# Subtracting the low part of every projection weight tile on GpSimd instead of VectorE

## The chip, the core and the metric

The kernel runs on one core of one Trainium2 chip. The metric is device time in microseconds (us) of one execution; several executions of a kernel are timed and their median is taken. Engines are named as the profile names them: PE is TensorE's matmul and PEld its weight load, DVE is VectorE, ACT is ScalarE, POOL is GpSimd, SP is SyncE, which here only issues DMAs.

## The reference, cut to what matters

One layer over 2064 tokens (16 learned meta tokens, then 2048) of 1024 numbers each:

```python
h = rmsnorm(x, norm_g)
p = h @ w_in                       # 1024 x 8208: the combined projection
qkv, z, a, b, sc_b, sc_c, sc_h, sc_z = split(p)
q, k, v = silu(causal_conv4(qkv))  # 8 heads of 128; q and k L2-normalised
o = chunk_gated_delta_rule(q, k, v, g(a), beta(b))
o_dn = rmsnorm(o) * silu(z)
o_sc = sc_b * causal_conv3(sc_c * sc_h) * silu(sc_z)
out = rmsnorm(x + concat(o_dn, o_sc) @ w_out)[16:]
```

The delta rule is a recurrence along the tokens with a triangular solve in each chunk. All inputs and outputs are float32.

## The kernel before

**Three products for one.** Matrix products run in the type `fp32r`. To keep float32 accuracy each operand is split: a high part (the value rounded to `fp32r`, written by ACT) and a low part (the value less its high part, again in `fp32r`). A product is then high x high + low x high + high x low, summed in PSUM. For a weight tile the three buffers are `wr` (raw, as loaded), `wh` (high) and `wl` (low), each 128 x 1024; the pool has two of each. For the tokens they are `hh` and `hl`.

**Jobs.** The projection is cut into 128 jobs: two halves of the sequence (`hf` 0 and 1), each 64 jobs of 128 columns of `w_in`, eight for each of eight heads (k, q, v, z of the delta group, then c, h, b, z of the short convolution). A job runs over three groups of tokens (272 or 256, 384, 384 columns); in each `run_group` issues 24 matmuls into one PSUM tile `mm`: 16 with `wh`, then 8 with `wl`. After the last group of job j, `split_w(j + 2)` issues the split of the weights of job j + 2: ACT copies `wr` to `wh`, and the subtraction `wl = wr - wh` follows. The loading of the weights of job j + 4 into the buffer `wr` just read (`load_w`, a DMA of 512 KB on SP's queue) is issued behind the subtraction.

**Two ways for the subtraction.** `split_w` has an argument `eng`. Without it the subtraction is cut into two halves of 512 columns, which are put into the list `side`; `pump` takes from that list when the planner thinks that DVE has little queued (`LAG`), and `side_until` empties it up to the half that a matmul is about to need. With `eng=nc.gpsimd` it is one POOL instruction over all 1024 columns, issued at once, with `load_w` right behind it. Before the change POOL has four: jobs 0 and 1, from the prologue, and the two jobs at the start of the second half (`POOLED`). The other 124 are on DVE.

**The order.** It is written out by the program itself: a planner (`Model`) keeps a clock for each engine with a cost for every kind of instruction (in `cost`: POOL's is 0.12 + n/445 us for a `tensor_tensor` of n columns) and the generators in `streams` yield until the planner says that their inputs are ready. Between the matmuls of a job, `pump` lets these generators issue the delta rule of the heads: `delta_front` (decay matrix E, Gram matrices of k and q, with the splits `gw`), `delta_inverse` (a triangular solve in 31 rows of two DVE instructions each, on `prod` and `XT`), `delta_back` (merging of blocks, on `W`, `X`, `Q`), `delta_scan` (the recurrence, 8 chunks a head, each with the DVE instructions `yy` and `S` between matmuls into `rec`), `delta_out` (normalisation, on `os`, and the gate `zs`). Every engine executes its own instructions strictly in the order issued. The planner has no term for two engines that hinder each other.

**POOL's other work.** The powers that stand for reciprocal roots (`opy`, `kpy`, `pxy`), the masks of `E` and `prod`, and two or three columns at the head of each convolution's buffer (`raw`, `sc_u`).

**The end.** When the jobs are done, 32 units of 48 matmuls multiply the mixed tokens with `w_out`. Their splits use the same pool tags `wr`, `wh`, `wl`, by ACT and DVE in `load_mix`; the change doesn't touch them.

Of the kernel before, what the change touches and what calls it, by code (L numbers as in the profile page):

```python
# [173 lines left out]
def hybrid_trunk(  # L174
# [544 lines left out]
    def split_w(j, eng=None):  # L719
        if j >= len(jobs):  # L720
            return
        J = jobs[j]
        J.wh = vt(wp, [128, KT, 128], "wh", dt=F32R)
        J.wl = vt(wp, [128, KT, 128], "wl", dt=F32R)
        nc.scalar.activation(J.wh, J.wr, AF.Copy)

        if eng is not None:
            eng.tensor_tensor(out=J.wl, in0=J.wr, in1=J.wh, op=ALU.subtract)
            load_w(j + 2)
            done.add(("w", j))  # L730
            return

        def half(i):
            s_ = slice(4 * i, 4 * i + 4)
            nc.vector.tensor_tensor(out=J.wl[:, s_], in0=J.wr[:, s_], in1=J.wh[:, s_], op=ALU.subtract)
            if i == 1:
                load_w(j + 2)

        later(lambda: half(0))
        later(lambda: half(1), ("w", j))  # L740

    def run_group(j, g):
# [25 lines left out]
        if g == 2:  # L768
            if J.fin:
                J.fin()  # L770
            split_w(j + 2, nc.gpsimd if j + 2 in POOLED else None)

# [739 lines left out]
        for l_ in sj:  # L1512
            jobs += l_
    NJ = len(jobs)
    POOLED = (NJ // 2, NJ // 2 + 1)
    HJ = NJ // 2
    start(prologue0())
    pump()
# [145 lines left out]
```

## Time and profile before

| | us |
|---|---|
| median of 3 runs | 2280.11 |
| lowest and highest | 2278.43, 2284.24 |
| the profiled execution | 2277.27 |
| its span, first to last instruction | 2275.5 |
| mean granted clock of TensorE, as a share of full speed | 0.985 |

The profile is of one execution. Its span lacks 1.8 us of that execution's own time, and the execution is 2.8 us below the median. A busy engine in it is one that executes an instruction; the idle time of an engine before an instruction is put down to what the instruction waited for. Nearly every instruction has the line 118, that of the helper that records it, so groups are told apart by the tiles they write and read.

### The profile page before, as it was taken

To read this page: it belongs to the slowest core of one execution; us is meant where nothing else is said; L and a number is where in the kernel's file an instruction comes from. 1 tells how busy PE (TensorE), PEld (TensorE's weight loads), DVE (VectorE), ACT (ScalarE), POOL (GpSimd) and SP (SyncE) were. 2 spreads that over 40 slices of the span, in tenths; PEclk is the share of its full clock that TensorE was granted. 3 is DMA by queue.
4 is the path that set the end of the run, shared out by engine and by line. 5 is a ranking of instruction groups with operands and counts; after the bars stand their busy time and mean duration, and the time that the engine had idled before them with its cause. 6 is when DMAs were issued, how large, how long until landed. Compare 5 with 4: busy or idle time off the path is not lost. (4 is left out here: it accounts for less than half of the span.)

```text
span 2275.5 us, 38771 instructions
## 1 busy us (share of the span) xinstructions
PE 2192.7 (96%) x15024; PEld 2071.2 (91%) x15024; DVE 1463.7 (64%) x4027; ACT 863.8 (38%) x2078; POOL 186.7 (8%) x343
## 2 busy tenths in 40 slices
PE   6999999999999998899999999999999999999998
PEld 6998899999998898889999999999999998788886
DVE  4667866777677657486877676776776775434222
ACT  5542444343434342344434343434352425322111
POOL 4010101010101010010100101010101000000000
PEclk9999899999999999999999999999999999999999
DMA  6443336534434478534443454243436864655231
GB/s 141 73 81 71 62 77 92 77 69 86 83 60 72 83 83 68 101 76 71 68 80 61 75 60 83 52 77 52 77 52 65 62 92 145 217 166 177 83 102 56
DMA packets 256518, 194.90 MB, mean 86 GB/s; under 512 B 62005, under 2 KB 226366, under 8 KB 256334
## 3 DMA queue, kind: packets, MB, share of 16 engines
q1 hardware_dynamic: 256334, 192.42, 46.5%
q8 instruction: 118, 1.93, 0.3%
q14 instruction: 66, 0.54, 0.1%
HBM read 156.58 MB, written 35.80 MB: 85 GB/s over the span
## 5 line engine op out<-in xcount | busy, mean ns | idle before, releaser
L118 PE MATMUL mm<-hh,wh 128*128 128x384 f32 (+3 forms) x3328 | 1046.3, 336 | 13.0 <-issue 6.7
L118 PE MATMUL mm<-hl,wh 128*128 128x384 f32 (+3 forms) x3328 | 1017.7, 327 | 0.0
L118 PEld LDWEIGHTS mm<-hh,wh 128*128 128x128 f32 x3328 | 630.4, 190 | 21.6 <-ACT hh L118 5.4
L118 PEld LDWEIGHTS mm<-hl,wh 128*128 128x128 f32 x3328 | 631.5, 191 | 16.5 <-issue 6.8
L118 PE MATMUL mm<-hh,wl 128*128 128x384 f32 (+3 forms) x3200 | 624.1, 327 | 6.9 <-DVE wl L118 6.9
L118 PEld LDWEIGHTS mm<-hh,wl 128*128 128x128 f32 x3200 | 512.0, 189 | 15.0 <-DVE wl L118 8.6
L118 DVE SCALAR_TENSOR_TENSOR acc<-raw,pcol,acc 128x384 f32<-128x384 f32 (+2 forms) x432 | 249.1, 580 | 76.3 <-ACT acc L118 70.9
L118 DVE TENSOR_TENSOR wl<-wr,wh 128x512 fp32r<-128x512 f32 x344 | 231.7, 694 | 100.9 <-ACT wh L118 58.8
L118 ACT ACTIVATE wh<-wr 128x1024 fp32r<-128x1024 f32 x176 | 185.7, 1055 | 106.1 <-PE mm L118 65.1
L118 DVE SCALAR_TENSOR_TENSOR prod<-nb,XT 128x8 f32<-128x8 f32 (+30 forms) x496 | 190.1, 383 | 24.4 <-DMA nb<-nbd 20.9
L118 DVE TENSOR_REDUCE XT<-prod 128x8 f32<-128x16 f32 (+30 forms) x496 | 147.2, 297 | 17.1
L118 ACT ACTIVATE raw<-mm 128x272 f32<-128x272 f32 (+2 forms) x144 | 65.7, 456 | 213.7 <-PE mm L118 213.1
L118 ACT ACTIVATE vn<-rec,cj 128x128 f32<-128x128 f32 x128 | 47.0, 367 | 226.3 <-PE rec L118 225.9
L118 ACT ACTIVATE sc_c<-mm 128x384 f32<-128x384 f32 (+4 forms) x99 | 45.1, 456 | 167.4 <-PE mm L118 167.3
L118 PE MATMUL mm<-oh,wh 128*128 128x512 f32 x256 | 101.9, 398 | 0.0
L118 PE MATMUL mm<-ol,wh 128*128 128x512 f32 x256 | 100.3, 392 | 0.0
L118 DVE TENSOR_TENSOR y<-mm,y 128x512 f32<-128x512 f32 x24 | 16.6, 692 | 115.9 <-PE mm L118 115.9
L118 POOL TENSOR_TENSOR opy<-mo,nhalf 128x4 f32<-128x4 f32 x32 | 35.7, 1116 | 648.6 <-DVE mo L118 592.7
L118 ACT ACTIVATE ojk<-y 128x512 bf16<-128x512 f32 x24 | 15.2, 632 | 191.6 <-DVE y L118 127.1
L118 DVE SCALAR_TENSOR_TENSOR yy<-rec,neg,vr 128x128 f32<-128x128 f32 x128 | 44.4, 347 | 60.8 <-PE rec L118 60.2
L118 ACT ACTIVATE acc<-mm,pcol 128x272 f32<-128x272 f32 (+2 forms) x144 | 78.2, 543 | 0.1
L118 DVE SCALAR_TENSOR_TENSOR S<-S,egl,rec 128x128 f32<-128x128 f32 x104 | 35.6, 343 | 61.0 <-PE rec L118 60.4
(244 smaller groups left out, 2596.1 us busy)
## 6 DMA issues: line engine op xcount, KB each, us to landing
wr<-in_w_in_dram SPq DMA_DIRECT2D x128, 512.0 KB, 9.0
wr<-mixd SPq DMA_DIRECT2D x48, 512.0 KB, 4.2
E<-gtd SPq DMA_DIRECT2D x16, 512.0 KB, 3.8
qd<-ged SPq DMA_DIRECT2D x16, 512.0 KB, 4.6
nb<-nbd SPq DMA_DIRECT2D x64, 128.0 KB, 4.3
mixd<-zs SPq DMA_DIRECT2D x32, 256.0 KB, 2.6
out_dram<-y SPq DMA_DIRECT2D x16, 512.0 KB, 2.7
mixd<-sc_y SPq DMA_DIRECT2D x32, 192.0 KB, 2.4
```

Of the source, the lines that this page charges most:

```text
L118: r = real(*args, **kw)
```

## The change

```diff
-    POOLED = (NJ // 2, NJ // 2 + 1)
+    POOLED = range(NJ)
```

`NJ` is 128. `POOLED` is read at one place, the last line of `run_group`: `split_w(j + 2, nc.gpsimd if j + 2 in POOLED else None)`. So for the jobs that had it on DVE (124 of them) the subtraction is now one POOL instruction of 1024 columns in place of two DVE halves of 512, the entries in `side` are gone, and `load_w(j + 2)` for that buffer is issued at once at the end of the job. Since the planner's clocks for DVE and POOL change with it, the order in which everything else is issued changes too.

## Rows read from the trace of the kernel before

**Rows 1.** The page, part 1: busy time, share and instructions of each engine.

```profile
PE 2192.7 (96%) x15024; PEld 2071.2 (91%) x15024; DVE 1463.7 (64%) x4027; ACT 863.8 (38%) x2078; POOL 186.7 (8%) x343
```

**Rows 2.** Stretches: busy us of PE, PEld, DVE, ACT, POOL; clock; DMA share; GB/s.

```profile
300.00:700.00 400.00, 396.01 (x2978) 385.28 (x2977) 282.39 (x856) 158.58 (x411) 35.75 (x67) 1.00 0.45 77
...
1000.00:1700.00 700.00, 696.94 (x5295) 680.61 (x5294) 505.69 (x1324) 291.86 (x727) 51.03 (x79) 1.00 0.41 67
```

**Rows 3.** PE's waits: us in total, times, longest.

```profile
PE mm L118 <- DVE wl L118: 6.9, 6, 4.0
```

**Rows 4.** Groups of instructions by shape: busy us, mean ns | idle before.

```profile
L118 DVE TENSOR_TENSOR wl<-wr,wh 128x512 fp32r<-128x512 f32 x344 | 231.7, 694 | 100.9 <-ACT wh L118 58.8 <-PE mm L118 35.8 <-PE rec L118 3.1
...
L118 POOL TENSOR_TENSOR wl<-wr,wh 128x1024 fp32r<-128x1024 f32 x4 | 9.5, 2381 | 16.9 <-ACT wh L118 16.9
```

**Rows 5.** DVE busy on tile wl alone, over the jobs' stretch; clock; DMA.

```profile
50.00:1905.00 1855.00, 170.48 (x250) 0.98 0.48 74
```

**Rows 6.** Timeline of POOL around 980 us: start, us, instruction.

```profile
974.84 2.39 POOL L118 TENSOR_TENSOR wl<-wr,wh 128x1024 fp32r<-128x1024 f32 x1 [7.71 <-ACT wh L118]
979.63 2.39 POOL L118 TENSOR_TENSOR wl<-wr,wh 128x1024 fp32r<-128x1024 f32 x1 [2.40 <-ACT wh L118]
981.96 0.22 POOL L118 COPY raw<-qcar 128x3 f32<-128x3 f32 x1
```

**Rows 7.** Timeline of DVE beside them.

```profile
975.28 0.69 DVE L118 TENSOR_TENSOR hl<-ta,hh 128x512 fp32r<-128x512 f32 x1 [1.39 <-ACT hh L118]
...
976.14 1.18 DVE L118 SCALAR_TENSOR_TENSOR prod<-nb,XT 128x80 f32<-128x80 f32 x1
...
978.90 0.15 DVE L118 SCALAR_TENSOR_TENSOR msm<-mnb,mXT 16x7 f32<-16x7 f32 x1
...
980.04 2.00 DVE L118 SCALAR_TENSOR_TENSOR msm<-mnb,mXT 16x8 f32<-16x8 f32 x1
```

**Rows 8.** Timeline of ACT: first, one middle and last of the 124 copies.

```profile
51.74 1.05 ACT L118 ACTIVATE wh<-wr 128x1024 fp32r<-128x1024 f32 x1
...
1425.78 1.06 ACT L118 ACTIVATE wh<-wr 128x1024 fp32r<-128x1024 f32 x1
...
1864.23 1.06 ACT L118 ACTIVATE wh<-wr 128x1024 fp32r<-128x1024 f32 x1 [3.50 <-PE mm L118]
```

**Rows 9.** Timeline of DVE behind the last two of these.

```profile
1427.11 0.40 DVE L118 SCALAR_TENSOR_TENSOR prod<-nb,XT 128x136 f32<-128x136 f32 x1
...
1865.45 0.16 DVE L118 SCALAR_TENSOR_TENSOR opt<-opt,mo 128x4 f32<-128x4 f32 x1
```

**Rows 10.** Three groups of DVE, by shape, that hand straight on to PE.

```profile
L118 DVE SCALAR_TENSOR_TENSOR yy<-rec,neg,vr 128x128 f32<-128x128 f32 x128 | 44.4, 347 | 60.8 <-PE rec L118 60.2
...
L118 DVE SCALAR_TENSOR_TENSOR S<-S,egl,rec 128x128 f32<-128x128 f32 x104 | 35.6, 343 | 61.0 <-PE rec L118 60.4
...
L118 DVE TENSOR_TENSOR gw<-q,gw 128x256 fp32r<-128x256 f32 x64 | 26.7, 418 | 0.0
```

**Rows 11.** Timeline of DVE: first and last of the 128 yy.

```profile
229.45 0.35 DVE L118 SCALAR_TENSOR_TENSOR yy<-rec,neg,vr 128x128 f32<-128x128 f32 x1
...
1938.16 0.35 DVE L118 SCALAR_TENSOR_TENSOR yy<-rec,neg,vr 128x128 f32<-128x128 f32 x1 [1.48 <-PE rec L118]
```

**Rows 12.** Timeline of PE: the matmuls that read these two.

```profile
231.23 0.38 PE L118 MATMUL rec<-yy,W 128*128 128x128 f32 x2
...
1939.55 0.38 PE L118 MATMUL rec<-yy,W 128*128 128x128 f32 x2
```

**Rows 13.** Three short stretches: columns as in the second group.

```profile
260.00:280.00 20.00, 14.54 (x66) 12.65 (x66) 18.68 (x53) 6.92 (x20) 1.25 (x1) 0.66 0.42 93
...
880.00:890.00 10.00, 5.06 (x20) 4.77 (x21) 9.62 (x30) 2.63 (x8) 0.00 (x0) 0.66 0.87 46
475.00:490.00 15.00, 13.23 (x91) 13.04 (x90) 10.75 (x54) 9.35 (x21) 1.30 (x3) 1.00 0.26 50
```

**Rows 14.** Waits of SP's DMA queue: us in total, times, longest.

```profile
SPq L118 <- DVE wl L118: 742.9, 151, 20.8
```

## The prediction, made before the changed kernel was run

> **What bounds the kernel now.** I read the page's busy shares first: PE is busy 96% of the span, DVE 64%, POOL 8% [rows 1]. Then the busy time by stretches, because a share of the whole span hides where the idle time lies: from 300 to 700 us PE idles for 4.0 of 400 us, from 1000 to 1700 us for 3.1 of 700 [rows 2]. In these stretches the matmuls are the time, and nothing that another engine does faster can shorten them. DVE idles there for 117.6 of 400 us and 194.3 of 700, that is 29% and 28% [rows 2]. Third, PE's own waits: in the whole execution PE waits for a low part of a weight on DVE six times, 6.9 us in all [rows 3]. So the subtractions that the change moves stand on the path for 6.9 us at most, though DVE spends 694 ns on each half [rows 4]. The reader should see that DVE is a loaded helper and not the bound, and that what counts is whether DVE's results for the delta rule come in time for the matmuls that are already queued in PE's fixed order.
>
> **What the change removes.** 124 jobs lose two DVE halves each: 248 x 694 ns = 172 us [rows 4], in line with the 170.5 us that DVE spends on `wl` between 50 and 1905 us [rows 5]. All of it lies beside PE's work but for the 6.9 us above; I count 0 for it directly, with 6.9 us of gain as the other end.
>
> **What it adds on POOL.** 124 subtractions of 2.381 us [rows 4] make 295 us, on an engine with 187 us of work [rows 1]. The copies of `wh` run from 51.7 to 1864.2 us [rows 8], so a job takes about 1812/124 = 14.6 us; copy and subtraction need 1.06 + 2.39 us of that, and the first matmul with this `wl` comes a whole job later. So PE should not wait for the subtraction itself: 0.
>
> **What it adds on DVE: being held.** Two of POOL's four subtractions ran beside a working DVE, from 974.84 and from 979.63 us, 2.39 us each [rows 6]. In the first, a DVE instruction with one input in PSUM (`hl<-ta,hh`) took its usual 0.69 us, but `prod<-nb,XT`, with both inputs in SBUF, took 1.18 us and ended at 977.32, right behind POOL's end at 977.23. In the second, `msm<-mnb,mXT`, at 0.15 us a little before, took 2.00 us and ended at 982.04, again with POOL (982.02) [rows 6, 7]. A larger `prod` (136 columns) takes 0.40 us undisturbed [rows 9]. So a DVE instruction that reads two operands in SBUF and begins during a POOL subtraction ends when POOL ends. The Trainium skill says the same (SBUF — State Buffer, section "Who interferes with whom"): such a DVE instruction contends with a GpSimd instruction that reads SBUF, and the loser blocks until the other is through. By that page the price is what is left of POOL's instruction, as these two rows have it; were the two engines independent, the sum below would lose its one positive term.
>
> I sized this by walking the timeline: for each of the 124 `wh` copies (the first, one between and the last are shown) [rows 8] a POOL subtraction of 2.39 us was laid right behind it, and the next DVE row with two inputs in SBUF, `wl` left out, was held until its end. Behind the copy at 1425.78 (ends 1426.84) POOL would run until 1429.28, and `prod` of 1427.11 would be held for 2.17 us; behind the last (ends 1865.29, POOL until 1867.73) `opt` of 1865.45 for 2.28 us [rows 8, 9]. In 20 of the 124 cases no such row begins in time. The sum over all is 189 us, 1.53 us a job; the two real cases, 0.8 us (1.18 less 0.40 at most for a smaller shape) and 1.85 us, have a mean of 1.3 us, or 164 us, and the ends are 0 and 124 x 2.39 = 296 us. I take 189: with 172 us removed, DVE gains nothing, and its work comes in gaps of up to 2.4 us which the planner doesn't know of.
>
> **What PE sees of it.** From the end of a `yy` to the matmul that reads it there are 231.23 - 229.80 = 1.43 us at the first and 1939.55 - 1938.51 = 1.04 us at the last of the 128; their median is 1.07 us [rows 11, 12]. A delay of DVE below that is free, and what lies above it stops PE. Of the 124 holds 92 are longer than 1.07 us, by 84 us in all. A delayed DVE catches up only in its idle time, 29% of the time [rows 2], so it is late by more than 1.07 us during 84/0.29 = 290 us. The DVE instructions that hand straight on to PE are 128 `yy`, 104 `S` and 64 pairs of `gw` [rows 10], 296 in 1855 us, one in 6.3 us; so 46 of them fall into late times, late by half of the mean excess (84/92/2 = 0.46 us): 21 us. This leaves out `os`, `X` and `W`. Moving every DVE row of the walk along, with catching up in the idle times, and letting PE wait where a matmul's input comes later than the matmul stands, gave 36 us at 56 places, 17 of them between 1000 and 1700 us, where PE now hardly waits. I take 32 us; the ends are 0 (no hold falls on a chain) and 84 (each does).
>
> **Clock.** PE's clock falls where PE is sparse for several microseconds: 0.66 from 260 to 280 us with 5.5 us of idle, 0.66 from 880 to 890; in a stretch with 1.8 us of idle (475 to 490) it stayed at 1.00 [rows 13]. The new waits are below 2.4 us and scattered, so I count 0; one more stretch of the first kind would cost 5.5 us of idle and 0.34 x 20 = 6.8 us of clock.
>
> **What it may give back.** In the two sparse stretches of rows 13 DVE is busy 18.7 of 20 and 9.6 of 10 us: PE has no matmul to issue because a head's delta rule is late. There are four such (also 725 to 740 and 770 to 780 us), with 17.8 us of idle and 0.34 x 55 = 18.7 us of clock. Fewer entries in `side` let the planner issue the solves earlier. But DVE's real load isn't less, so I take 6 us of the 36.
>
> **What is moved in the queues.** On POOL, the copies into the head of `raw` now wait for a subtraction, as the one at 981.96 us did [rows 6]; behind a late copy DVE's `acc`, and with it `prod` and `yy`, would be held. In the walk a few first readers stand before the copy's end, by less than 0.8 us: 0 to 4 us, taken as 0. POOL's powers and masks wait for up to 2.39 us more, and the planner knows it (its formula gives 2.42 us); 0. POOL in turn waits for `wh`, as ACT's copy ends it. On SP's queue `load_w` is issued earlier, and everything behind it waits until POOL has read `wr`: 1.06 + 2.39 us and ACT's queue behind a job's end, 4 to 5 us. Now SP waits for DVE's halves for 742.9/151 = 4.9 us a time [rows 14]. So 0, within 8 us either way, since the transfers of `nb` that start a solve stand in that queue.
>
> **Sum.** The profiled execution took 2277.3 us: + 32 - 6 = 2303 us. The median is 2.8 us above that execution: **2306 us**, 1.1% slower.
>
> **Rivals.** *The heads run ahead.* If the solves, freed of the halves in between, finish some 5 us earlier, the four sparse stretches vanish (-36 us), and if the chains, issued earlier, gain slack so that only a third of the holds' cost is left (+11 us), the time is 2280 - 25 = 2255 us; in part, up to 2272. It decides from the point where a job no longer waits for the scan of the head before last. For it: DVE is full there. Against it: the holds fall on just these instructions, `prod` above all. *Nothing moves.* The holds stay within the slack of 1.07 us or cancel against the relief: 2274 to 2287, say 2280 us. The Trainium skill has a sentence for this (Perfetto Trace Analysis, section "Optimizing Scalar/DVE Operations"): offloading between these two engines may not help, as they share a read port; the trace agrees so far as 172 us stand against 189. *The sparse stretches multiply.* Where DVE is already above 90% a hold isn't caught up, and a head's delta rule is late for the next job. Four more stretches of 12.3 us on top of the 32 give 2280 + 32 + 49 = 2361 us. For it: heads in the first half have the `msm` rows in addition. Against it: from 1000 to 1700 us DVE has 28% to spare.
>
> **How the numbers follow.** The forecast, 2288 to 2340 us, has 0.57, the multiplied stretches (above 2340) 0.08, nothing moved 0.16, the heads ahead 0.19. A measurement of this kernel can tell about 0.3% (7 us) from no change. So slower has 0.65, same 0.16, faster 0.19. The range that leaves out half of the two outer cases is 2262 to 2345 us.
>
> **What would show it.** In the profile after, DVE's busy time should be about as before (1464 - 172 + 189 = 1481 us) though 248 instructions are gone, with `prod`, `acc` and `junk` longer on average; POOL near 480 us; PE's waits for DVE `S`, `yy`, `gw` and `os`, and PE's idle time between 1000 and 1700 us well above 3 us, with the clock near 1.00 there. If DVE is busy for 1300 us, the holds are wrong. If it is near 1480 us and PE idles no more than now, the slack is wrong. If the four sparse stretches are gone, the first rival is right.

## The result and the profile after

| | before | after |
|---|---|---|
| median, us | 2280.44 | 2341.84 |
| lowest and highest, us | 2278.43, 2284.24 | 2341.07, 2347.2 |
| span of the profiled execution, us | 2275.5 | 2339.4 |
| PE's idle time in it (span less busy), us | 82.8 | 127.8 |
| mean granted clock of TensorE | 0.985 | 0.982 |

The changed kernel takes 1.0272 times as long, 95% interval 1.0252 to 1.0293: 61 us more, where 26 were forecast. The direction was right. The time lies 2 us above 2340 us, where the forecast's main case ends, and 3 us below the upper end of the wide range (2262 to 2345 us).

The page of the kernel after, part 1, answers [rows 1]; its stretches (busy us of PE, PEld, DVE, ACT, POOL; clock; DMA share; GB/s) answer [rows 2].

```profile
PE 2211.6 (95%) x15024; PEld 2078.3 (89%) x15024; DVE 1494.1 (64%) x3783; ACT 861.7 (37%) x2078; POOL 494.0 (21%) x467
...
300.00:700.00 400.00, 383.10 (x2867) 369.06 (x2866) 279.45 (x782) 151.25 (x396) 99.70 (x86) 0.99 0.43 74
700.00:1000.00 300.00, 276.66 (x1977) 268.01 (x1976) 200.33 (x570) 117.95 (x304) 72.47 (x71) 0.96 0.63 86
1000.00:1700.00 700.00, 668.86 (x4925) 646.65 (x4926) 486.76 (x1198) 268.33 (x667) 163.73 (x125) 0.99 0.39 63
```

DVE has lost 244 instructions and is busy 30 us longer than before. PE's idle time from 300 to 700 us went from 4.0 to 16.9 us, from 1000 to 1700 us from 3.1 to 31.1 us: the stretches in which PE hardly waited are where the time went. (The stretches are the same in microseconds and not in work; a count by work stands with the experiments.)

PE's waits in the kernel after (us in total, times, longest):

```profile
PE rec L118 <- DVE os L118: 22.9, 12, 8.3
PE ta L118 <- DVE gw L118: 19.1, 15, 4.0
PE rec L118 <- DVE yy L118: 12.4, 14, 2.7
PE ta L118 <- DMA W<-xtd: 7.8, 2, 6.0
PE rec L118 <- DVE S L118: 7.8, 9, 1.7
PE ta L118 <- DVE X L118: 7.3, 12, 2.9
```

PE waits for the delta rule's results. The wait for the low part of a weight [rows 3] is gone, but it was 6.9 us.

Groups of DVE and POOL by line and tile (count | busy us, mean ns | idle before), with the lengths mixed in `acc`, `prod` and `XT`; first two from the page of the kernel before:

```profile
L118 DVE SCALAR_TENSOR_TENSOR acc<-raw,pcol,acc 128x384 f32<-128x384 f32 (+2 forms) x432 | 249.1, 580 | 76.3 <-ACT acc L118 70.9
...
L118 DVE SCALAR_TENSOR_TENSOR prod<-nb,XT 128x8 f32<-128x8 f32 (+30 forms) x496 | 190.1, 383 | 24.4 <-DMA nb<-nbd 20.9
```

and of the kernel after:

```profile
L118 DVE SCALAR_TENSOR_TENSOR acc<-raw,pcol,acc 128x384 f32<-128x384 f32 (+2 forms) x432 | 300.5, 698 | 89.1 <-ACT acc L118 78.5 <-POOL raw L118 6.2
L118 DVE SCALAR_TENSOR_TENSOR prod<-nb,XT 128x8 f32<-128x8 f32 (+30 forms) x496 | 235.4, 475 | 21.9 <-DMA nb<-nbd 17.8
L118 DVE TENSOR_REDUCE XT<-prod 128x8 f32<-128x16 f32 (+30 forms) x496 | 147.2, 297 | 17.1
...
L118 DVE SCALAR_TENSOR_TENSOR yy<-rec,neg,vr 128x128 f32<-128x128 f32 x128 | 44.4, 347 | 82.7 <-PE rec L118 81.8
...
L118 POOL TENSOR_TENSOR wl<-wr,wh 128x1024 fp32r<-128x1024 f32 x128 | 316.4, 2472 | 1075.7 <-ACT wh L118 933.9
```

The same `acc` and `prod` instructions now take 51 and 45 us more. `XT<-prod` (a reduction of one input) and `yy` (one of its two inputs in PSUM) take what they took, 147.2 and 44.4 us. One hold, with the matmul behind it, on the timeline of the kernel after:

```profile
1626.90 3.26 DVE L118 SCALAR_TENSOR_TENSOR acc<-raw,pcol,acc 128x384 f32<-128x384 f32 x2
...
1627.10 2.65 POOL L118 TENSOR_TENSOR wl<-wr,wh 128x1024 fp32r<-128x1024 f32 x1 [13.46 <-ACT wh L118]
...
1630.08 0.34 DVE L118 SCALAR_TENSOR_TENSOR yy<-rec,neg,vr 128x128 f32<-128x128 f32 x1
...
1630.48 0.49 PE L118 MATMUL rec<-yy,W 128*128 128x128 f32 x2 [0.97 <-DVE yy L118]
```

Two `acc` run from 1626.90 to 1630.16 us, where one takes 0.58 us on the mean in the kernel before (249.1/432). The first begins before POOL and takes its usual 0.61 us; the second begins at 1627.54 and ends 0.4 us behind POOL (1629.75), 2.62 us in all; `yy` stands behind them in DVE's queue, and PE idles 0.97 us for `yy`.

### The profile page after: what moved, and what is told of

The parts are those of the page before. It is cut to its first block, busy times and chain, and to the rows that moved or that the text cites. A ratio compares the mean times of both kernels' runs of the same rounds, so it can differ in the third digit from the quotient of the medians.

```text
span 2339.4 us, 38650 instructions
## 1 busy us (share of the span) xinstructions
PE 2211.6 (95%) x15024; PEld 2078.3 (89%) x15024; DVE 1494.1 (64%) x3783; ACT 861.7 (37%) x2078; POOL 494.0 (21%) x467
## 4 chain that ended last, share of the span: by engine, by line
PE 34%; DVE 12%; DMA 3%; ACT 2%; issue 2%; SPq 1%; POOL 1%; POOLq 0%; ACTq 0%; DVEq 0%
PE mm L118 28%; DVE prod L118 4%; DVE acc L118 3%; PE ta L118 3%; DVE XT L118 2%; PE rec L118 2%; SPq L118 1%; PE o L118 1%; DMA nbd<-E 1%; DMA xtd<-XT 1%; ACT junk L118 1%; DMA nb<-nbd 1%; DVE sc_y L118 1%; POOL wl L118 1%; DMA E<-gtd 1%
## 5 line engine op out<-in xcount | busy, mean ns | idle before, releaser
L118 PE MATMUL mm<-hh,wl 128*128 128x384 f32 (+3 forms) x3200 | 631.6, 330 | 0.0
L118 POOL TENSOR_TENSOR wl<-wr,wh 128x1024 fp32r<-128x1024 f32 x128 | 316.4, 2472 | 1075.7 <-ACT wh L118 933.9
L118 PEld LDWEIGHTS mm<-hh,wl 128*128 128x128 f32 x3200 | 519.8, 192 | 6.8 <-issue 0.4
L118 DVE SCALAR_TENSOR_TENSOR acc<-raw,pcol,acc 128x384 f32<-128x384 f32 (+2 forms) x432 | 300.5, 698 | 89.1 <-ACT acc L118 78.5
L118 DVE SCALAR_TENSOR_TENSOR prod<-nb,XT 128x8 f32<-128x8 f32 (+30 forms) x496 | 235.4, 475 | 21.9 <-DMA nb<-nbd 17.8
L118 DVE TENSOR_REDUCE XT<-prod 128x8 f32<-128x16 f32 (+30 forms) x496 | 147.2, 297 | 17.1
L118 DVE TENSOR_TENSOR wl<-wr,wh 128x512 fp32r<-128x512 f32 x100 | 65.2, 687 | 51.5 <-PE mm L118 29.7
L118 DVE SCALAR_TENSOR_TENSOR yy<-rec,neg,vr 128x128 f32<-128x128 f32 x128 | 44.4, 347 | 82.7 <-PE rec L118 81.8
L118 PE MATMUL ta<-gw 128*128 128x256 f32 x384 | 62.5, 292 | 21.9 <-DVE gw L118 19.1
L118 PEld LDWEIGHTS ta<-gw 128*128 128x128 f32 x384 | 53.6, 192 | 28.8 <-DVE gw L118 23.0
```

The costliest lines, as they stand in the source:

```text
L118: r = real(*args, **kw)
```

## The experiments

"Memsets" below: POOL writes `wl` twice with a constant (0.96 us each, no input) between two subtractions of one column, about as long as a subtraction, so that DVE is hardly held; the low parts of the weights are then missing from the products. A time is a median, a ratio is to the kernel before in the same runs, with its 95% interval. The kernel before moved from 2280 to 2285 us between the sets of runs, so a difference of two medians from different sets is uncertain by some 7 us. The diffs are shortened; in them `gp` is `tc.nc.gpsimd`, `tc.nc` issues an instruction that the planner doesn't book, and `model.issue` books one that isn't issued.

That two kernels have the same order means that the instructions of PE, DVE and ACT stand in the same sequence. SP's do not always: between the kernel after and e9 its DMA issues stand in the same order too, but between the kernel after and e1 25 of 714 stand elsewhere, between e2 and e5 18 of 709, between e17 and e18 64. What is called the price of the holds below contains what this does.

**Order and holds apart.** The change does two things: it holds DVE, and it gives the planner other clocks, so other orders. Four kernels separate them: either order, with subtractions or memsets.

```diff
 # e1_nolock: the changed kernel's order, memsets
-eng.tensor_tensor(out=J.wl, in0=J.wr, in1=J.wh, op=ALU.subtract)
+gp.tensor_tensor(wl[one column], wr, wh); gp.memset(J.wl, 0.0)
+gp.memset(J.wl, 0.0); gp.tensor_tensor(wl[one column], wr, wh)
+model.issue("POOL", 0.12 + 1024 / 445.0, [J.wl], [J.wr, J.wh])
 # e2_oldorder: in half(i) of the kernel before
-nc.vector.tensor_tensor(out=J.wl[:, s_], in0=J.wr[:, s_], in1=J.wh[:, s_], op=ALU.subtract)
+model.issue("DVE", 0.066 + 512 / 960.0, [J.wl], [J.wr, J.wh])
+if i == 1: tc.nc.gpsimd.tensor_tensor(out=J.wl, in0=J.wr, in1=J.wh, op=ALU.subtract)
 # e5_oldnolock: as e2, memsets for the subtraction
```

> The order of the changed kernel, to the instruction, with POOL busy as long but without long reads: the 1024-column subtraction on POOL is replaced by a one-column subtraction, two memsets of the low part and the one-column subtraction again, while the planner still books 2.42 us. The low parts of the weights are left out of the computation (they are zero but for a column). Theory of the holds (DVE instructions with two operands in SBUF stand still while POOL reads): DVE's busy time falls to about 1300 us, PE's waits fall back to some 50 us and the time to 2270 to 2290 us. Rival, the order (what the planner reissued, the earlier load of the raw weights in SP's queue, the copies behind the subtraction): the time stays at 2325 to 2345 us.

> The order of the kernel before, as its planner still books the two halves on DVE, but the subtraction itself is one POOL instruction of 1024 columns, put where the second half stood; the raw weights are reloaded behind it as before. Theory of the holds: DVE is held for about as long as in the changed kernel (190 us), and the time is 2305 to 2345 us. Of this 2312 us is what the walk of the prediction gave for just this order (2280 + 32). Rival, the order: 2275 to 2290 us, as nothing is reissued.

> The order of the kernel before; in place of POOL's one subtraction a job (run e2_oldorder) one column of it, two memsets and the column again, as in e1_nolock; the low parts of the weights are left out (zero but for a column). DVE has neither the halves nor the holds. It parts what the order gave in e1_nolock (28 us below before) from what the freed DVE gave. If the relief comes from DVE's freed time: 2250 to 2265 us, and the holds of e2_oldorder cost 90 us. If it comes from the new order: 2275 to 2287 us, and the holds of e2_oldorder cost 70 us.

| | no holds | holds | holds cost |
|---|---|---|---|
| before's order | e5: 2287.67 (1.0021, 1.0003 to 1.0038) | e2: 2351.95 (1.0288, 1.0259 to 1.0316) | 64 us |
| the changed order | e1: 2256.69 (0.9868, 0.9843 to 0.9893) | after: 2341.84 (1.0272) | 85 us |

Part 1 of the pages of e1, e2 and e5:

```profile
PE 2186.2 (97%) x15024; PEld 2067.0 (92%) x15024; DVE 1323.1 (59%) x3783; ACT 861.4 (38%) x2078; POOL 475.7 (21%) x851
```
```profile
PE 2223.8 (94%) x15024; PEld 2091.0 (89%) x15024; DVE 1506.8 (64%) x3779; ACT 865.5 (37%) x2078; POOL 494.6 (21%) x467
```
```profile
PE 2198.2 (96%) x15024; PEld 2075.7 (91%) x15024; DVE 1326.6 (58%) x3779; ACT 863.8 (38%) x2078; POOL 481.3 (21%) x839
```

The holds are DVE's difference in one order: 1494.1 - 1323.1 = 171 us in the changed one, 1506.8 - 1326.6 = 180 us in the old. By the ratios in place of the medians the holds cost 61 and 92 us. Freeing DVE of 172 us in the old order gives nothing (e5), nor does leaving out the low parts, which e5 does too. e1 came out 13 us below its range and e2 7 us above. The new order gives 2287.67 - 2256.69 = 31 us where DVE isn't held; with holds it gives 10, and the two intervals overlap.

Where the 85 us go: e1's span is 2255.0 us, so PE idles there for 68.8 us, after the change for 127.8, 59 us more; for the other 25 us PE is busy longer, of which the lower clock, 0.982 against 0.990, makes an estimated 20 us (0.018 x 2339 - 0.010 x 2255). In the old order the profiled executions of e2 and e5 are 73 us apart, 47 of idle time and 26 of longer work. Cut into sixteen stretches of 192 matmuls that read `wl`, about one for each head's jobs in each half, PE idles longer after the change than in e1 in every one, by 0.6 to 6.9 us: the loss is spread evenly. PE's waits in e1 (us in total, times, longest) and two of its stretches:

```profile
PE rec L118 <- DVE os L118: 16.3, 5, 7.3
...
PE rec L118 <- DVE yy L118: 3.8, 2, 3.0
...
PE ta L118 <- DVE gw L118: 1.5, 1, 1.5
```
```profile
700.00:1000.00 300.00, 287.47 (x2060) 276.67 (x2059) 193.98 (x632) 124.60 (x310) 68.45 (x123) 0.98 0.64 84
1000.00:1700.00 700.00, 687.05 (x5190) 671.57 (x5190) 437.40 (x1198) 284.27 (x722) 165.38 (x277) 0.99 0.42 65
```

`gw` and `yy` carry 26 us of waiting in the kernel after that is not in e1; `S` adds 7 us, `os` 7 and the transfer of `W` 8. From 700 to 1000 us, where three of the four sparse stretches lay, PE idles for 12.5 us in e1 and for 23.3 after the change, at clock 0.98 and 0.96.

**e12_unbooked: the books alone.** The halves stay on DVE, but the planner books no time for them.

```diff
-nc.vector.tensor_tensor(out=J.wl[:, s_], ...)
+tc.nc.vector.tensor_tensor(out=J.wl[:, s_], ...); model.issue("DVE", 0.0, [J.wl], [J.wr, J.wh])
```

> The kernel before, with both halves on DVE, but the planner books no time on DVE for them, only the wait for their inputs. No hold by POOL, and the planner's books are wrong by some 1.2 us of DVE's time a job (167 us in all), as they are wrong by the holds (171 us) in the changed kernel. If any DVE time that isn't in the books costs the same: about 2320 to 2345 us. If a hold costs more than ordinary work because it stops DVE at a place that the planner can't choose, while the halves stand in the list where there is room: 2265 to 2295 us, and below 2280 it would beat both kernels.

2290.48 us, ratio 1.0016 (1.0002 to 1.003). Fewer booked microseconds without a freer DVE give nothing in this order, which is not quite the changed one; with e5 this speaks for a relief that needs both.

**Every other job.** Half of the subtractions on POOL, as they are and as memsets.

```diff
-    POOLED = range(NJ)
+    POOLED = (*range(0, NJ, 2), NJ // 2 + 1)
```

> Every other job has its subtraction on POOL (65 jobs), the rest on DVE in halves as before. Theory of the holds: about half the loss, 2305 to 2318 us. Rival, a threshold (the loss comes only where DVE is full, and half the load relieves it): 2275 to 2290 us.

> As e4_half (every other job on POOL), with POOL's subtractions replaced by one column, two memsets and the column again; the low parts of those weights are left out. Theory that each us of hold costs the same, about half a us, however long the single hold is (85 us for 171 us of hold in the changed kernel, 49 for 90 in e3_chop4): DVE's busy time falls by about 80 to 90 us against e4_half and the time by 40 to 48 us, to 2248 to 2257 us. Rival, that long holds cost more than short ones: more than 55 us, below 2241 us. Rival, that half the holds find cover: less than 25 us, above 2271 us.

e4 took 2296.49 us, ratio 1.0051 (1.0037 to 1.0065); e6 2270.55, ratio 0.9942 (0.9927 to 0.9957). Half the change has 26 us of cost for its holds (DVE busy 1473.5 - 1391.3 = 82 us, so 0.32 us for each us) against 13 us of relief: the same two effects, smaller, with the price above the gain again. Both times lie outside what either theory gave for e4 and just outside the last one for e6.

**The planner is told.** After each subtraction the planner takes DVE as busy until POOL has ended.

```diff
+model.free["DVE"] = max(model.free["DVE"], model.free["POOL"])
```

> The changed kernel, but the planner books DVE as taken until POOL's subtraction ends, so that it issues DVE work of the delta rule, and the matmuls behind it, later. If the loss comes from the planner's not knowing of the holds: PE's waits fall to some 70 us and the time to 2285 to 2310 us. Rival, that the loss is DVE's lost time itself, at whatever place the planner puts the work: 2325 to 2350 us.

> The order of e7_told (the planner books DVE as taken until POOL is through; 2430 us) with POOL's subtractions replaced by one column, two memsets and the column, so that nothing is held; the low parts of the weights are left out. If that order is itself the loss: 2340 to 2400 us. If the holds cost in it what they cost in the changed kernel and there is more of them: 2280 to 2320 us.

e7 took 2429.7 us, ratio 1.064 (1.0622 to 1.0657); e11, the same order with memsets, 2392.98, ratio 1.0481 (1.0448 to 1.0513). Both theories for e7 missed. Foreseen this way, the holds (DVE busy 1453.2 - 1312.0 = 141 us) cost 37 us instead of 85, but the order made for them costs over 100 us by itself. Why it costs so much was not followed further.

**Size.** The subtraction in four or eight pieces that the planner books one by one (e3, e8: other orders), in four pieces in the changed kernel's order (e9), and twice over in that order (e10).

```diff
 # e9_chop4same; e3 and e8 use eng.tensor_tensor without the last line; e10: the whole subtraction twice
-eng.tensor_tensor(out=J.wl, in0=J.wr, in1=J.wh, op=ALU.subtract)
+for i in range(4):
+    s_ = slice(2 * i, 2 * i + 2)
+    tc.nc.gpsimd.tensor_tensor(out=J.wl[:, s_], in0=J.wr[:, s_], in1=J.wh[:, s_], op=ALU.subtract)
+model.issue("POOL", 0.12 + 1024 / 445.0, [J.wl], [J.wr, J.wh])
```

> The changed kernel with each POOL subtraction cut into four of 256 columns, some 0.7 us each. Theory of the holds with a slack (a hold shorter than the 1.07 us between a DVE result and its matmul is free): the longest single hold is 0.7 us, PE's waits fall to some 55 us and the time to 2280 to 2300 us, though POOL reads for longer in all. Rival, the total (it is the sum of DVE's lost time that counts, not the length of one hold): 2330 us or more. Rival, the order: 2330 to 2345 us.

> The changed kernel with each POOL subtraction cut into eight of 128 columns, some 0.4 to 0.5 us each. If the cost goes with the sum of the holds: it falls only as far as DVE's busy time falls; with holds of 60 to 90 us in all, 2285 to 2305 us. If a single hold below the slack were free: 2257 to 2270 us.

> The changed kernel with POOL's subtraction in four pieces of 256 columns, while the planner books one of 1024 as before: the order on PE, DVE and ACT is that of the changed kernel, which e3_chop4 did not keep. Without any hold this order takes 2257 us (e1_nolock), with whole holds 2342. If the cost goes with the sum of the holds (about 90 us in e3_chop4 against 171): 2290 to 2305 us. If single holds below the slack of about 1 us are free: 2257 to 2272 us. If the length of a hold made no difference: 2335 us or more.

> The changed kernel with each POOL subtraction executed twice in a row, booked once; same order on PE, DVE and ACT. POOL reads for twice as long. If the cost goes with the sum of the holds, half a us for each us: DVE's busy time rises by 130 to 170 us and the time by 65 to 85 us, to 2405 to 2430 us. If it grows faster than the sum, since a delay that isn't caught up adds to the next: above 2440 us. If the second subtraction finds DVE waiting anyway: below 2380 us.

e3 2306.04 us, ratio 1.0083 (1.0059 to 1.0107); e8 2347.9, 1.0279 (1.0263 to 1.0296); e9 2314.25, 1.0135 (1.0118 to 1.0152); e10 2560.85, 1.1192 (1.1152 to 1.1232). The pages of e9 (part 1, and POOL's group) and e10 (part 1):

```profile
PE 2199.2 (95%) x15024; PEld 2073.4 (90%) x15024; DVE 1417.4 (61%) x3783; ACT 863.9 (37%) x2078; POOL 592.3 (26%) x851
...
L730 POOL TENSOR_TENSOR wl<-wr,wh 128x256 fp32r<-128x256 f32 x512 | 422.6, 855 | 987.5 <-ACT wh L118 880.3 <-PE rec L118 55.1 <-PE ta L118 16.5
```
```profile
PE 2288.2 (89%) x15024; PEld 2143.2 (84%) x15024; DVE 1686.7 (66%) x3783; ACT 863.5 (34%) x2078; POOL 815.1 (32%) x595
```

e3, e8 and e9 lie outside what their theories gave. e3 and e8 have no run of their own order without holds; e8's DVE is busy for 1372.0 us only, so why it is the slowest of the three stays open.

e9 against the kernel after is the cleanest pair: the order is the same on PE, DVE, ACT and SP, and only POOL's subtraction is cut. 77 us less of hold (1494.1 - 1417.4) make the time 28 us shorter, although POOL works 98 us longer.

e9 is also the test of the prediction's slack. A piece takes 0.855 us on the mean; of the DVE rows beside one 267 are over 0.06 us longer than the median of their shape in the traces without holds, two of them by more than 1.07 us, and the median is 0.42 us. By "below that is free" the time would be e1's, 2257 us. It is 58 us more, for 1417.4 - 1323.1 = 94 us of hold. Adding up the holds of the four pieces of a job doesn't save the rule: in 46 of 128 jobs the sum is above 1.07 us, by 22 us in all. e10, where the highest of the three ranges came true, has 1686.7 - 1323.1 = 364 us of hold and costs 304 us, but part of that need not be hold, as the next runs show.

**POOL's own queue, and gaps.** Perhaps the four holds of e9 add up because they come back to back. In e13 and e14 POOL writes a small tile four or eight times between two pieces; e15 is as long as e14 with memsets in place of the pieces.

```diff
 # e13_spaced (4), e14_spaced_more (8): behind each of the first three pieces of e9
+for _ in range(4): tc.nc.gpsimd.memset(spacer, 0.0)   # 128 x 128
 # e15_long_nohold: e1, with 24 of these between its two memsets
 # e16_..., e17_..., e18_long_heads_on_act: as e9, as e13, and as e15 with 12, and in each
-nc.gpsimd.tensor_copy(raw[:, 0:3], qcar[:, t, :])
+tc.nc.scalar.activation(raw[:, 0:3], qcar[:, t, :], AF.Copy)
-nc.gpsimd.tensor_copy(sc["u"][:, 0:2], ucar[:, s, :])
+tc.nc.scalar.activation(sc["u"][:, 0:2], ucar[:, s, :], AF.Copy)
```

> The changed kernel's order; POOL's subtraction in four pieces of 256 columns, and between two pieces four memsets of a 128 x 128 tile that nothing reads, so that a DVE instruction with two inputs in SBUF that was held by one piece can run on before the next. The four pieces back to back cost 57 us above the same order without subtractions (2314 against 2257 us), although hardly one held instruction was late by more than 1.07 us. Theory A (a burst of short holds adds up because DVE has no time between them to catch up): with the gaps the cost falls by a third or more, to 2290 us or less, with the held time at most equal. Theory B (each us of hold costs the same wherever it lies, about 0.6): the time follows the held time alone; with 94 us of it, 2314 us, and as much less as DVE's busy time falls.

> As the run before, with eight memsets between two pieces. Theory A: lower again, towards 2270 us, below the kernel before. Theory B: as the run before by its held time, near 2314 us. If POOL's own lateness counts (its copies into the head of the convolution's buffers wait behind the longer sequence), the time rises instead, and DVE's acc waits for POOL longer.

> The changed kernel's order without the subtractions (low parts of the weights left out), with 24 memsets of the 128 x 128 tile between the two that stand for a subtraction: as long a sequence on POOL as in the run before, with nothing in it that holds DVE. If POOL's lateness costs nothing: 2257 us, as without them. What lies above 2257 us is the price of the longer sequence and is to be taken off the run before.

They took 2393.07 us, ratio 1.048 (1.0446 to 1.0515), 2645.81, 1.1582 (1.1557 to 1.1608), and 2600.79, 1.1386 (1.1365 to 1.1406). Neither theory A nor B fits e13; e14 rose, as its third case says. e15, without the holds, loses 344 us against e1. The waits of DVE on POOL in e15 (us, times, longest), and POOL's timeline:

```profile
DVE acc L118 <- POOL raw L118: 243.7, 43, 8.7
...
DVE sc_y L118 <- POOL sc_u L118: 64.3, 15, 6.2
DVE XT L118 <- POOL prod L118: 60.6, 10, 10.3
```
```profile
1427.95 6.23 POOL L734 MEMSET spacer<- 128x128 f32 x24
1434.12 0.95 POOL L735 MEMSET wl<- 128x1024 f32 x1
1435.15 0.19 POOL L736 TENSOR_TENSOR wl<-wr,wh 128x1 fp32r<-128x1 f32 x1
1435.28 0.19 POOL L118 COPY raw<-qcar 128x3 f32<-128x3 f32 x1
```

A copy of three columns, 0.19 us, stands behind the sequence in POOL's queue, and the convolution's `acc`, with all of DVE's queue behind it, waits for the copy. This price is separate from the holds, and it had to go before gaps could be judged: ACT does these copies in e16 to e18.

> Four pieces back to back in the changed kernel's order (2314 us), and the copies of two or three columns into the heads of raw and sc_u, which stood behind the pieces in POOL's queue, on ACT. In the four-piece kernel DVE waited 29 us for these copies. Theory A (POOL's queue matters where the subtraction is short or cut): 5 to 25 us less, 2290 to 2309 us. Theory B (only the holds matter): 2314 us within 7. DVE's waits for POOL on raw vanish in either case.

> The four pieces with four memsets between two of them, and the same copies on ACT. The spaced kernel with the copies on POOL took 2393 us, with 139 us of DVE's waiting for them, and its 24-memset relative without holds 2601 us, so the longer sequence on POOL has a price of its own. Theory A (the copies carry most of that price): below 2330 us. Its cost of the holds is the difference to the next run: if a burst of short holds adds up and gaps relieve it, under 38 us; if each us of hold costs about 0.6, some 40 to 55 us.

> The control of the run before: the changed kernel's order without the subtractions (low parts of the weights left out), 12 memsets of the 128 x 128 tile between the two that stand for a subtraction, the copies on ACT. No holds. If the copies were the whole price of the longer sequence: 2257 us within 10. If POOL's masks and powers, which also wait in its queue, carry a share: 2270 to 2310 us.

e16 took 2305.69 us, ratio 1.0102 (1.0075 to 1.0129), 9 us less than e9, though the two intervals overlap; e17 2330.31, 1.0204 (1.0182 to 1.0225), 63 us less than e13; e18 2282.43, 0.999 (0.9978 to 1.0001). So in e13 the copies carry 63 us of the longer sequence's price, and 26 us over e1 are left in e18, whose DVE still waits 44 us for the masks of `prod` (18 in e1). Part 1 of the pages of e17 and e18:

```profile
PE 2209.8 (95%) x15024; PEld 2082.6 (90%) x15024; DVE 1413.3 (61%) x3783; ACT 868.2 (37%) x2142; POOL 847.5 (36%) x2323
```
```profile
PE 2188.9 (96%) x15024; PEld 2067.6 (91%) x15024; DVE 1318.2 (58%) x3783; ACT 867.3 (38%) x2142; POOL 766.6 (34%) x2323
```

e17 against e18: 1413.3 - 1318.2 = 95 us of hold cost 48 us. With gaps of about 0.9 us between them short holds cost 0.50 us for each us; back to back (e9) 0.61, with POOL's sequence 0.8 us longer than e1's; whole (after) 85/171 = 0.50. Each is uncertain by 0.04 to 0.07, so they are hardly told apart: gaps of this size relieve little and make nothing free. In e14 against e15, where POOL's queue has long used up the slack, 58 us of hold cost 45 us, 0.78.

No version with the subtractions on POOL came below the kernel before; the nearest was e4.

## Why the prediction was right in direction and too small

**The holds: right.** 189 us were forecast; the same order with and without shows 171. DVE's busy time is 1494 us (1481 forecast), POOL's 494 (480). The rows of the kernel after show the mechanism of [rows 7] on `acc` and `prod`, and a reduction of one input and rows with one input in PSUM unchanged. The excess was sized right as well: beside POOL's subtractions 92 DVE rows of the kernel after are more than 1.07 us longer than the median of their shape, by 84 us in all, the very figures of the walk (95 and 87 us in e2, which has the order that the walk used). As the Trainium skill has it (SBUF — State Buffer, section "Who interferes with whom"), a DVE instruction with two inputs in SBUF contends with a POOL instruction that reads SBUF and not with one that only writes it: in e1, with memsets, `prod` takes 191.7 us against 190.1 before the change.

**What PE sees of it: the step that failed.** It priced the 84 us of excess at 32: a delay below 1.07 us is free, and one above it counts only where it meets a hand-over to PE. The runs show 64 us in the old order and 85 in the new. In the profiled executions PE's idle time makes 47 of 73 and 59 of 84 us of this, and the clock of the next point most of the rest. e9 refutes the first half of the rule: holds that are nearly all shorter than 1.07 us cost 0.61 us for each us. The waits speak against the second half: `yy`, `S` and `gw` alone gained 34 us against e1, where the count by late times had 21, and `os`, `X` and `W`, which that count left out by name, gained 16 more. The walk along the rows, made in the old order, had 36 us where the idle time grew by 47. (`os` has the largest wait of the kernel after, 22.9 us, but 16.3 of it are there without holds.) What would have come near, as one sees afterwards, is the whole sum of the holds times a third to a half (64/180 = 0.36 in the old order, 0.50 in the new; 26/82 = 0.32 in the pair of every other job). Why short holds reach PE is argued and not shown: a solve is a chain of 31 rows, so several short holds on it reach PE as one long delay, whatever the slack of a single hand-over.

**Clock: taken as 0, some 15 to 20 us.** The step rested on new waits that are short and scattered. Short they are in the changed order: PE's stops of 0.3 to 2.4 us come to 72 us in the kernel after and to 19 in e1, those above 2.4 us to 37 and 31. The clock fell all the same. Its mean, between TensorE's two levels of 1.2 and 2.4 GHz, is 0.990 without holds and 0.982 with them in the changed order, 0.982 and 0.973 in the old one: an estimated 20 and 23 us of the profiled spans, and 18 and 15 by the median clocks of all runs. Against the kernel before, whose clock is 0.985, the change loses 42 - 34 = 8 us.

In the old order long waits grew as well. One place of e2, which has the order of the kernel before; first the timeline of before, then that of e2:

```profile
1740.28 0.17 DVE L118 SCALAR_TENSOR_TENSOR prod<-nb,XT 128x8 f32<-128x8 f32 x1 [8.99 <-DMA nb<-nbd]
...
1742.26 0.15 DVE L118 TENSOR_TENSOR opt<-opy 128x4 f32<-128x4 f32 x1
...
1743.58 1.11 PE L118 MATMUL rec<-ident,os 128*128 128x128 f32 x4 [5.27 <-DVE os L118]
```
```profile
1804.66 0.17 DVE L118 SCALAR_TENSOR_TENSOR prod<-nb,XT 128x8 f32<-128x8 f32 x1 [12.30 <-DMA nb<-nbd]
...
1806.64 2.15 DVE L118 TENSOR_TENSOR opt<-opy 128x4 f32<-128x4 f32 x1
...
1809.96 1.11 PE L118 MATMUL rec<-ident,os 128*128 128x128 f32 x4 [11.00 <-DVE os L118]
```

`opt` is held, 2.15 us in place of 0.15, and PE idles 11.00 us behind it in place of 5.27. The hold has 2.00 us of that. Most of the rest is the first row of the solve, which waits for its transfer for 12.30 us in place of 8.99, and that this is a hold's doing is not shown: in e5 the same row waits for no transfer, and the DMA issues around it stand in another order.

**What it may give back: right in kind, too small.** 6 us were taken; the new order without holds gives 24 us against the kernel before as it ran beside the change, 29 as it ran beside e1, and 31 against e5. The rival of the heads that run ahead named this mechanism, and once DVE is free the order does part of what it says: from 700 to 1000 us PE idles 12.5 us in e1, 23.8 before. That e1 took 2257 us and the rival said 2255 is luck: the rival counted 36 us of relief and 11 us of holds, and e1 has less relief and no holds. One of its four stretches was also read wrongly: from 770 to 780 us DVE is busy for 7.2 of 10 us and not full. What refutes it for this change is its own "against": holds fall on `prod` and `acc`, and from 700 to 1000 us the idle time returns to 23.3 us.

**POOL's queue: small here, not small in general.** The copies were taken as 0 to 4 us; DVE waits 6.2 us for them in the kernel after, and 14.0 us for the masks of `prod` against 4.3 before. In e1, where DVE is hardly held and comes to them sooner, it waits 29.5 us for the copies, so in the kernel after a part of this queue is hidden behind the holds. At 2.4 us a subtraction just fits; in e13, with about 6 us of POOL's work a job, the queue costs 63 + 26 us and the holds 48.

**The sum.** Where it had -6 for what is given back and +32 for the holds, the runs show -24 and +85, clock included: +61 (by the ratios -30 and +92). The rival "nothing moves" is out by the interval. That of the multiplied stretches (2361 us, above 2340) comes nearer in size, for a wrong reason: from 700 to 1000 us PE idles 23.3 us, 23.8 before; the loss lies where DVE has 30% to spare, 13 us of idle from 300 to 700 and 28 us from 1000 to 1700, and against e1 it is spread over all heads.

## What to carry to other kernels

An instruction that is taken off a loaded helper engine gives nothing if its new place holds that helper for as long: test it with a stand-in of the same length that doesn't touch the disputed resource, which tells the gain of the order from the price of the holds. Look whether the DMA queue's order stayed the same too. Do not call a delay free because it is shorter than the slack of one hand-over; in this kernel a us of held time cost 0.3 to 0.6 us as long as POOL's queue kept up, and a first guess elsewhere may start there. And before an in-order engine gets a long instruction, list the tiny ones that others wait for behind it.

## What was not expected of the hardware

- POOL is slowed as well: its 1024 columns took 2.47 us on the mean in the kernel after, 2.38 in the four cases before [rows 4]. At 1627.10 it took 2.65 us, beside the `acc` that had begun 0.2 us earlier and was not held itself. Four pieces of 256 took 4 x 0.855 = 3.42 us.
- The hold isn't a matter of a long POOL instruction: pieces of 256 columns, 0.8 us each, still hold DVE for 94 us in all.
- The hold also reaches a DVE instruction with one tensor as input, `sc_y<-sc_u` with a constant for each partition: 48 of them took 20.2 us before and 29.1 after. These rows of the kernel after show one free and one held until about POOL's end (1548.55). `XT<-prod`, a reduction with one input, was not held. The Trainium skill has this too (SBUF — State Buffer, section "Who interferes with whom"): `tensor_scalar` may run in a mode that takes both port pairs, a reduction never does. In which mode these rows ran is not shown. The prediction's walk left them out.

```profile
1540.45 0.42 DVE L118 TENSOR_SCALAR sc_y<-sc_u,pcol 128x384 f32<-128x384 f32 x1
...
1546.62 2.15 DVE L118 TENSOR_SCALAR sc_y<-sc_u,pcol 128x384 f32<-128x384 f32 x1
...
1546.16 2.39 POOL L118 TENSOR_TENSOR wl<-wr,wh 128x1024 fp32r<-128x1024 f32 x1 [4.49 <-ACT wh L118]
```

- These one-input rows are also held by POOL's memsets, which hold no `prod`: in e1 the 48 `sc_y<-sc_u` take 23.1 us, 20.2 before, and the 16 `ssk<-ssk` 4.3 us, 2.7 before. So the kernels with memsets are not quite free of holds; in e1 they come to about 7 us. The rows of e1:

```profile
L118 DVE SCALAR_TENSOR_TENSOR prod<-nb,XT 128x8 f32<-128x8 f32 (+30 forms) x496 | 191.7, 387 | 26.6 <-DMA nb<-nbd 22.6
...
L118 DVE TENSOR_SCALAR sc_y<-sc_u,pcol 128x384 f32<-128x384 f32 (+2 forms) x48 | 23.1, 480 | 1.3 <-POOL sc_u L118 0.3
...
L118 DVE TENSOR_SCALAR ssk<-ssk 128x8 f32<-128x8 f32 x16 | 4.3, 270 | 0.6
```
